# Down-projection weight sums: from VectorE through SBUF to copying and adding transfers within DRAM

## The chip, the cores and the metric

The kernel runs on one core of a Trainium2 chip. The metric is the device time of one execution in microseconds; the program uses only this core, so there is no slowest core to look for. Lower is better.

## The reference, cut to what matters

The program is a two-layer decoder trunk on a residual stream of 512 tokens by 1024 features in float32. Layer 0 has dilated windowed attention (12 heads in three groups, with rotary embedding), layer 1 has forgetting attention (16 heads, with keys and values computed once between the layers). Each is followed by a gated feed-forward block, and the change touches the last product of that block, the down-projection:

```python
def conv_ffn(xn, w_up, cw, cb, w_down):
    a = xn @ w_up
    T = a.shape[1]
    ap = jnp.pad(a, ((0, 0), (CONV_W - 1, 0), (0, 0)))
    a = sum(ap[:, j:j + T] * cw[j] for j in range(CONV_W)) + cb
    gate, val = jnp.split(a, 2, axis=-1)
    return (jax.nn.gelu(gate, approximate=True) * val) @ w_down     # (512, 2816) @ (2816, 1024)
```

## The kernel before

Every product is done in three float32r matmuls (high by high, high by low, low by high), so each weight piece of 128 x 1024 is loaded from DRAM by SyncE (`Weights.load`, L50), split into a high part on ScalarE and a low part on VectorE, and then used by TensorE. The emission order of the code is the order on each engine; nothing is rescheduled. A wait therefore holds up everything that stands behind it on the same engine's queue.

The down-projection works on eleven pairs `j` of 128-row chunks of `w_down[l]`, by a seven-product scheme (Strassen's, in Winograd's form): the 2 x 2 blocks of a pair (rows in two chunks of 128, columns in two halves of 512) are combined into four sums, the activations into matching sums (`pair_sums`, `pair_two`), and `combine_one` puts the products together. The weight sums don't depend on the data, so they are made long before they are used, and kept in a DRAM tensor `dT[l]` of 11 x 128 x 2048 floats. `down_sums` is a generator: each `next` emits one step of it.

* Before, one pair costs three loads into two SBUF tiles `dsums` (L615 to L617, SyncE), four subtractions of 128 x 512 on VectorE (L625) and two stores of 128 x 1024 to `dT` (L607, from SyncE or GpSimd).
* The steps stand between other work: the eleven pairs of layer 0 and pairs 6, 7 and 8 of layer 1 in the QKV stage of layer 0; pairs 0 to 5 of layer 1 in the stage that computes the shared keys and values; pairs 9 and 10 at the end of the forgetting attention.

Two places outside `down_sums` matter for the prediction:

* In the QKV stage, `wide_proj` makes one column group in four steps of weight pieces. After the last one `qk_post` scales the result on ScalarE and applies the rotary embedding on GpSimd, four instructions for each of four token blocks (L1139 to L1142). TensorE then transposes these blocks (`qk_transpose`, L1148).
* In the forgetting attention, `f_mask` (L1701) applies the causal mask to a bias tile on GpSimd; `f_exp` on VectorE (L1727) reads it, and `f_transpose` on TensorE (L1751) reads what comes out two units later. The first mask stands directly behind the last step of `down_sums` of the key and value stage on GpSimd's queue.

DMAs issued by SyncE (queue q1) and by GpSimd (queue q0) are carried by the same 16 DMA engines. GpSimd already issues adding transfers in the feed-forward blocks (`accum_op=ALU.add`, from one SBUF tile into another, L98 and L715), and the plain stores of `hD` (L671).

Of the kernel before, what the change touches and what calls it, by code (L numbers as in the profile page):

```python
# [13 lines left out]
ALU = mybir.AluOpType  # L14
# [16 lines left out]
ND = NF // 2  # L31
# [86 lines left out]
def trunk_kernel(ctx, tc, x, norm_gains, w_qkv_a, w_o_a, w_q_b, w_o_b, kv_norm, w_kvf, b_f,  # L118
# [11 lines left out]
    def t8(shape, dt=F32, name="t8"):  # L130
        return p8.tile(shape, dt, tag="t8", name=name)
# [22 lines left out]
    def add(f):  # L154
        pieces.append(f)
# [25 lines left out]
    def add_ffn(l):  # L181
        for c in range(NF):
            add_cols(w_up[l], c * 128)
            add_cols(w_up[l], DFF + c * 128)

        for j in range(ND):
            add(lambda raw, j=j: [(raw[:, 0:512], w_down[l][j * 256:j * 256 + 128, 0:512]),
                                  (raw[:, 512:1024], dT[l][j, :, 0:512])])
            add(lambda raw, j=j: [(raw, dT[l][j, :, 512:1536])])
        add_rows(w_down[l], range(1, NF, 2))  # L190

    add_rows(w_o_a[0], range(6))
# [403 lines left out]
        dve.tensor_copy(cp, pc)  # L596
        return cp

    def down_sums(pairs, place, queue, lag, behind, steps=False):


        live, n = [], len(pairs)

        def store(i):
            l, j = pairs[i]
            for q, t in enumerate(live[i]):
                queue.dma_start(dT[l][j, :, q * 1024:q * 1024 + 1024], t)  # L607

        for i in range(n + lag + behind):
            if i < n:  # L610
                l, j = pairs[i]
                a, b = place()
                live.append((a, b))
                r = w_down[l][j * 256:j * 256 + 256, :].rearrange("(c p) d -> c p d", p=128)
                sp.dma_start(a, r[0])  # L615
                sp.dma_start(b[:, 0:512], r[1, :, 512:1024])
                sp.dma_start(b[:, 512:1024], r[1, :, 0:512])  # L617
            single = steps and i - lag == n - 1
            if single:
                store(i - lag - behind)  # L620
            if 0 <= i - lag < n:
                a, b = live[i - lag]
                a0, a1, b0, b1 = a[:, 0:512], a[:, 512:1024], b[:, 0:512], b[:, 512:1024]
                for o, p, m in ((a0, a1, a0), (a1, b0, a1), (b0, b0, a0), (b1, b1, b0)):
                    dve.tensor_tensor(o, p, m, ALU.subtract)  # L625
                    if single and o is not b1:
                        yield
            if i >= lag + behind and not single:
                store(i - lag - behind)
            yield  # L630

    def in_one():
        t = t8([128, 2, 1024], name="dsums")
        return t[:, 0], t[:, 1]

    def in_two():
        return [t4([128, 1024], name="dsums") for _ in range(2)]

    def ffn(l, bd, cp, nxt, ahead):
        hD = tc.dram_tile([NF, 128, T], F32, name="hD")
# [144 lines left out]
        def pair_sums(j):  # L792

            pair_load(j + 1)
            k = acts[j]
            dve.tensor_tensor(k[:, s3_], k[:, a11], k[:, s1_], ALU.subtract)
            dve.tensor_tensor(k[:, s1_], k[:, s1_], k[:, s2_], ALU.add)
            dve.tensor_tensor(k[:, s2_], k[:, s1_], k[:, a11], ALU.subtract)
            pool.dma_start(sD[j], k[:, s2_])

# [11 lines left out]
        def load_two(j):  # L812

            if j < ND:
                later2[j] = k, r4 = t4([128, 768], name="dact2"), t2([128, 512], name="dt4")
                sp.dma_start(k[:, 0:256], sD[j])
                sp.dma_start(k[:, 256:768], hD[2 * j + 1])
                sp.dma_start(r4, dT[l][j, :, 1536:2048])
# [26 lines left out]
        def mul_one(j, bp):  # L845
            wa, wb, ac = [(t[:, 0], t[:, 1]) for t in one[j]]

            for key, q, w, c in (((bp, 0), 0, wa, H[0]), ((bp, 1), 3, wb, H[1]),
                                 ((bp + 2, 0), 2, wb, H[0]), ((bp + 2, 1), 1, wa, H[1])):
                if j == 0:  # L850
                    db[key] = bank([128, 512], name="acc")
                product_of(db[key], ac, q, w, c, bp, j == 0)

        def combine_one(bp):
            a, b, c, d = db[bp, 0], db[bp, 1], db[bp + 2, 0], db[bp + 2, 1]
            p1, u, u3 = (t2([128, 512], name="dsum") for _ in range(3))
            act.copy(p1, a)
            dve.tensor_tensor(u, b, p1, ALU.add)
            dve.tensor_tensor(c, c, u, ALU.add)
            act.copy(u3, c)  # L860
            dve.tensor_tensor(b, d, u, ALU.add)
            dve.tensor_tensor(d, d, u3, ALU.add)


        def p_11(j, bp, part=slice(0, 512)):
# [361 lines left out]
    def factors():  # L1227
# [9 lines left out]
        for _ in range(2):  # L1237
            next(down0)
# [193 lines left out]
    next(sums)  # L1432
# [18 lines left out]
    def v_post(g, b, o):  # L1451
        if b == 0:
            for i in (1, 2):
# [5 lines left out]
    v_proj0([[L(qk_transpose, 0, 0), L(qk_transpose, 0, 1), L(next, down0)],  # L1459
             [L(qk_transpose, 0, 2), L(qk_transpose, 0, 3), L(scores, 0, 0, 1), L(next, sums), L(next, down0)]])  # L1460
    wide_proj(1, "qk_ps", qk_post, [
        [],
        [L(scores, 0, 2, 3), L(next, sums)],
        [L(next, sums)],
        [stat_out, L(next, sums)]])
    wide_proj(2, "qk_ps", qk_post, [
        [L(next, sums)],
        [L(f, g, b) for f, g in ((p_transpose, 0), (qk_transpose, 1)) for b in range(4)],
        [L(scores, 1, 0, 1, 2, 3)],
        [exps, stat_in]])  # L1470
# [1 line left out]
    wide_proj(1, "v_ps", v_post, [  # L1472
        [L(qk_transpose, 2, 0), L(qk_transpose, 2, 1)],
        [L(qk_transpose, 2, 2), L(qk_transpose, 2, 3), L(scores, 2, 0, 1)],
        [L(next, down0), L(next, down0), L(scores, 2, 2, 3), factors],
        []], (0, 1, 3))
    pv(0, 0)
    for b in range(4):
        p_transpose(1, b)
# [120 lines left out]
    for sp_, b in [(sp_, b) for b in bd2.order for sp_ in (0, 2)]:  # L1600
# [14 lines left out]
    del wv  # L1615
    next(down1)

    bia = {}
# [39 lines left out]
    for c in range(8):  # L1658
        keys(c)
        for kc in range(2 * c, min(2 * c + 2, KD)):  # L1660
            if kc % 4 == 0:
                for part, name in zip(xTq, ("xqh", "xql")):
                    part.append(t8([128, 4, T], F32R, name=f"{name}{kc // 4}"))
            bd2.second(xTq, kc)
        if 1 <= c <= 5:
            next(gate)
        if c in (0, 1):
            next(down1)
# [139 lines left out]
    for n in range(N + 3):  # L1808
# [14 lines left out]
        if live:  # L1823
            if n + 1 < N:
                f_mask(*units[n + 1])
            if i == 1:
                q_low(j + 1)
            if i == 2 and j < 2 or (j, i) in ((6, 2), (7, 1)):
                W.low()
            if i == 3 and j:  # L1830
                f_out_low(j - 1)
            if i != 2:
                q_part(j + 1 + (i > 0), (i + 3) % 4)
            if (j, i) in ((7, 1), (7, 2)):
                next(down1)
        if 2 <= n < N + 2:
            f_transpose(*units[n - 2])
        if live and i == 1 and 2 <= j < 6:
# [19 lines left out]
    for _ in range(2):  # L1858
        next(down1)
    f_out_low(7)  # L1860
    W.ahead, W.ahead_dma = 4, 2
    cp = conv_columns(load_conv(1))
# [47 lines left out]
```

## Time and profile before

| | |
|---|---|
| time, median of 3 runs | 1097.54 us (1097.53 to 1097.63) |
| profiled execution: span | 1095.3 us |
| TensorE busy | 1088.0 us, 99% |
| TensorE weight loads busy | 946.4 us, 86% |
| VectorE busy | 882.3 us, 81% |
| ScalarE busy | 667.5 us, 61% |
| GpSimd busy | 154.4 us, 14% |
| DMA, of 16 engines' span | q1 (SyncE) 53.6%, q0 (GpSimd) 20.3% |

The profiled execution has no time of its own besides its span of 1095.3 us; the median of the runs stands 2.2 us above it, for what lies ahead of the first and behind the last instruction. The granted TensorE clock is 0.998 of full speed. GpSimd's DMA-issuing instructions are counted as its busy time; SyncE's are not.

### The profile page before, as it was taken

How to read it: one execution, taken by the hardware profiler on the slowest of the kernel's cores; microseconds unless marked ns; L12 is line 12 of the kernel's file. 1: busy time of each engine (PE TensorE's matmuls, PEld its weight loads, DVE VectorE, ACT ScalarE, POOL GpSimd, SP SyncE). 2: the span in 40 equal slices, each digit the busy share in tenths (PEclk: the TensorE clock that was granted, in tenths of full speed). 3: DMA queues.
4: the chain of work that ended last, by engine and by line, in shares of the span. 5: the costliest groups of instructions: out<-in, count | busy, mean ns of one | idle time of the engine just before them, and what ended most of it. 6: DMA issues, size and time to landing. Idle time of an engine off the chain costs nothing.

```text
span 1095.3 us, 17965 instructions
## 1 busy us (share of the span) xinstructions
PE 1088.0 (99%) x6537; PEld 946.4 (86%) x6537; DVE 882.3 (81%) x1510; ACT 667.5 (61%) x1117; POOL 154.4 (14%) x240
## 2 busy tenths in 40 slices
PE   9999999999999999999999999999999999999997
PEld 7888889899999988888878888889899999988886
DVE  5898979877878789897686667858878788779895
ACT  6745665656666656576451587755755656647473
POOL 2643000111111111000001212100111111211000
PEclk9999999999999999999999999999999999999999
DMA  9899944668898979793447867784568978979872
GB/s 292 241 366 405 351 125 135 135 164 198 190 210 190 226 266 325 268 341 99 146 143 240 274 174 207 243 238 136 105 174 190 213 184 184 245 244 318 313 250 77
DMA packets 191984, 241.60 MB, mean 221 GB/s; under 512 B 12832, under 2 KB 139160, under 8 KB 191896
## 3 DMA queue, kind: packets, MB, share of 16 engines
q1 hardware_dynamic: 176552, 189.33, 53.6%
q0 software_dynamic: 14656, 51.13, 20.3%
q8 instruction: 51, 0.84, 0.3%
q14 instruction: 37, 0.30, 0.1%
q10 hardware_dynamic: 688, 0.01, 0.1%
HBM read 172.37 MB, written 39.73 MB: 194 GB/s over the span
## 4 chain that ended last, share of the span: by engine, by line
PE 95%; DMA 2%; issue 1%; DVE 1%; ACT 0%; SPq 0%; DVEq 0%; ACTq 0%; POOL 0%; POOLq 0%
PE up L294 12%; PE up L292 12%; PE up L293 12%; PE acc L292 9%; PE acc L294 9%; PE acc L293 9%; PE v_ps L293 2%; PE v_ps L292 2%; PE v_ps L294 2%; PE pT_ps L1751 2%; PE o_ps L1766 2%; PE s_ps L1717 2%; PE qk_ps L292 1%; PE first L292 1%; PE first L293 1%; PE first L294 1%
## 5 line engine op out<-in xcount | busy, mean ns | idle before, releaser
L292 PE MATMUL acc<-w 128*128 128x512 f32 (+1 forms) x311 | 120.5, 388 | 0.0
L294 PE MATMUL acc<-w 128*128 128x512 f32 (+1 forms) x311 | 120.4, 387 | 0.0
L293 PE MATMUL acc<-w 128*128 128x512 f32 (+1 forms) x267 | 103.2, 387 | 0.0
L292 PE MATMUL up<-xsh,w 128*128 128x256 f32 x352 | 99.6, 283 | 0.0
L293 PE MATMUL up<-xsl,w 128*128 128x256 f32 x352 | 99.6, 283 | 0.0
L294 PE MATMUL up<-xsh,w 128*128 128x256 f32 x352 | 99.6, 283 | 0.0
L655 ACT ACTIVATE bb<-up,conv 128x512 f32<-128x512 f32 x80 | 59.7, 776 | 59.2 <-DVE up L1046 48.4
L60 ACT CAST w<-wraw 128x1024 fp32r<-128x1024 f32 x81 | 83.2, 1051 | 18.6 <-DMA wraw<-in_w_up_dram 7.8
L294 PE MATMUL up<-xch,w 128*128 128x512 f32 (+1 forms) x276 | 93.5, 339 | 0.1
L292 PE MATMUL up<-xbh,w 128*128 128x512 f32 (+1 forms) x276 | 93.6, 339 | 0.0
L293 PE MATMUL up<-xcl,w 128*128 128x512 f32 (+1 forms) x276 | 93.5, 339 | 0.0
L293 PE MATMUL up<-xbl,w 128*128 128x512 f32 (+1 forms) x276 | 93.5, 339 | 0.0
L292 PE MATMUL up<-xch,w 128*128 128x512 f32 (+1 forms) x276 | 93.5, 339 | 0.0
L294 PE MATMUL up<-xbh,w 128*128 128x512 f32 (+1 forms) x276 | 93.4, 338 | 0.0
L78 DVE TENSOR_TENSOR w<-wraw,w 128x1024 fp32r<-128x1024 f32 x62 | 74.6, 1223 | 16.6 <-ACT w L60 16.2
L292 PEld LDWEIGHTS acc<-w 128*128 128x128 f32 x311 | 58.4, 188 | 11.9
L294 PEld LDWEIGHTS acc<-w 128*128 128x128 f32 x311 | 58.4, 188 | 11.8
L292 PEld LDWEIGHTS up<-xsh,w 128*128 128x128 f32 x352 | 67.6, 192 | 0.0
L293 PEld LDWEIGHTS up<-xsl,w 128*128 128x128 f32 x352 | 67.6, 192 | 0.0
L294 PEld LDWEIGHTS up<-xsh,w 128*128 128x128 f32 x352 | 67.6, 192 | 0.0
L656 DVE SCALAR_TENSOR_TENSOR bb<-up,conv,bb 128x511 f32<-128x511 f32 x80 | 59.5, 744 | 7.9 <-ACT bb L655 7.8
L98 POOL DMA_DIRECT2D w<-wraw x20 | 17.5, 876 | 336.8 <-ACT w L71 307.3
(317 smaller groups left out, 3112.8 us busy)
## 6 DMA issues: line engine op xcount, KB each, us to landing
wraw<-in_w_up_dram SPq DMA_DIRECT2D x88, 512.0 KB
w<-wraw POOLq DMA_DIRECT2D x32, 512.0 KB, 6.2
dT<-dsums SPq DMA_DIRECT2D x28, 512.0 KB
dsums<-in_w_down_dram SPq DMA_DIRECT2D x22, 512.0 KB
dsums<-in_w_down_dram SPq DMA_DIRECT2D x44, 256.0 KB
w<-wsum POOLq DMA_DIRECT2D x22, 512.0 KB, 5.6
hD<-hc POOLq DMA_DIRECT2D x44, 256.0 KB, 7.2
dact<-hD SPq DMA_DIRECT2D x44, 256.0 KB
```

The source lines that it names most:

```text
L60: (copy or self.nc.scalar.copy)(pair[:, 0], raw)
L78: self.nc.vector.tensor_tensor(pair[:, 1], raw, pair[:, 0].bitcast(F32), ALU.subtract)
L98: self.nc.gpsimd.dma_start(pair[:, 1], raw, accum_op=ALU.add)
L292: pe.matmul(o, ah, bh, start=first, stop=False, skip_group_check=shared)
L293: pe.matmul(o, ah, bl, start=False, stop=False, skip_group_check=shared)
L294: pe.matmul(o, al, bh, start=False, stop=last, skip_group_check=shared)
L655: act.activation(bb[:, s, :], ps, AF.Identity, bias=cp[:, 3, ch:ch + 1], scale=cp[:, 2, ch:ch + 1])
L656: dve.scalar_tensor_tensor(bb[:, s, 1:], ps[:, :T - 1], cp[:, 1, ch:ch + 1], bb[:, s, 1:], ALU.mult, ALU.add)
L1717: pe.matmul(sc[j, i][hh][:, :nn], qT[j][own, qp, i * 128:(i + 1) * 128], k[own, kp, :nn], start=qp + kp == 0, stop=qp == 1)
L1751: pe.transpose(o[:, k0 + k, :], p[:, hh, k * 128:(k + 1) * 128], ident)
L1766: pe.matmul(o[64 * hh:64 * hh + 64, i * 128:(i + 1) * 128], Vt[hd // 8][:, k, (hd % 8) * 64:(hd % 8) * 64 + 64], pT[j, i, hh][:, k, :], st ...
```

## The change

The sums are no longer made on VectorE. For each pair, two transfers of SyncE copy the four blocks from `w_down` straight into the four sections of `dT`, one of the blocks twice (`twice` reads it with a step of zero). Three adding transfers of GpSimd then finish the sums within DRAM: the second block of the first chunk is added into sections 0 and 3, section 3 into section 2, and section 2 into section 1. Each is one step of the generator later than the one that it depends on, so pair `i` takes steps `i` to `i + 3`, and eleven pairs take 14 steps. The transfers add where VectorE subtracted, so two of the sums have the opposite sign, and the activations' sums and `combine_one` are changed to match. The sections of `dT` change places accordingly. All pairs of layer 0 are now made in the QKV stage (14 steps), all of layer 1 in the key and value stage (14 steps), and the steps at other places are gone.

```diff
-    def down_sums(pairs, place, queue, lag, behind, steps=False):
+    def twice(a):
+        return bass.AP(tensor=a.tensor, offset=a.offset, ap=[a.ap[0], [0, 2], a.ap[1]])
+
+    def down_sums(pairs):
+        n = len(pairs)
+        sums = [dT[l][j].rearrange("p (s c) -> p s c", c=512) for l, j in pairs]
+
+        def rows(i, c):
             l, j = pairs[i]
...
-                a, b = place()
-                live.append((a, b))
-                r = w_down[l][j * 256:j * 256 + 256, :].rearrange("(c p) d -> c p d", p=128)
-                sp.dma_start(a, r[0])
-                sp.dma_start(b[:, 0:512], r[1, :, 512:1024])
-                sp.dma_start(b[:, 512:1024], r[1, :, 0:512])
...
-                for o, p, m in ((a0, a1, a0), (a1, b0, a1), (b0, b0, a0), (b1, b1, b0)):
-                    dve.tensor_tensor(o, p, m, ALU.subtract)
...
+            return w_down[l][j * 256 + c * 128:j * 256 + c * 128 + 128, :]
+
+        for i in range(n + 3):
             if i < n:
+                sp.dma_start(sums[i][:, 0::2], twice(rows(i, 0)[:, 0:512]))
+                sp.dma_start(sums[i][:, 1::2], rows(i, 1).rearrange("p (s c) -> p s c", c=512))
+            if 0 <= i - 1 < n:
+                pool.dma_start(sums[i - 1][:, 0::3], twice(rows(i - 1, 0)[:, 512:1024]), accum_op=ALU.add)
+            if 0 <= i - 2 < n:
+                pool.dma_start(sums[i - 2][:, 2], sums[i - 2][:, 3], accum_op=ALU.add)
+            if i - 3 >= 0:
+                pool.dma_start(sums[i - 3][:, 1], sums[i - 3][:, 2], accum_op=ALU.add)
             yield
...
-            dve.tensor_tensor(k[:, s1_], k[:, s1_], k[:, s2_], ALU.add)
+            dve.tensor_tensor(k[:, s1_], k[:, s1_], k[:, s2_], ALU.subtract)
...
-            dve.tensor_tensor(k[:, 0:256], k[:, 256:512], k[:, 0:256], ALU.subtract)
+            dve.tensor_tensor(k[:, 0:256], k[:, 256:512], k[:, 0:256], ALU.add)
...
-    sums = down_sums([(1, 6), (1, 7)], in_two, sp, 1, 3)
...
-    down0 = down_sums([*[(0, j) for j in range(ND)], (1, 8)], in_one, sp, 1, 1, True)
+    down0 = down_sums([(0, j) for j in range(ND)])
...
-    down1 = down_sums([(1, j) for j in range(6)], in_two, pool, 1, 0)
+    down1 = down_sums([(1, j) for j in range(ND)])
...
-    down1 = down_sums([(1, 9), (1, 10)], in_one, pool, 2, 0)
```

The number of matmuls and their order on TensorE are the same. What moves is on GpSimd, SyncE and VectorE. On GpSimd in the QKV stage, before, the rotary embedding of column group 1 (`qk_811`) follows directly on the casts of the stage's beginning, and that of group 2 (`qk_1126`) directly on that:

```order
L1122 CAST xph_142<-xah_138 128x16x32
L1122 CAST xpl_144<-xal_140 128x16x32
L1139 TENSOR_TENSOR rope<-qk_811,rope 128x128
L1140 TENSOR_TENSOR rope<-qk_811,rope 128x8x8
L1141 TENSOR_TENSOR rope<-qk_811,rope 128x8x8
L1142 TENSOR_TENSOR qk_811<-rope 128x8x16
```

Now (the same instructions have the lines L1101 and L1118 to L1121, the groups the names `qk_770` and `qk_1061`, and `dT_75` is `dT` of layer 0) nine adding transfers stand ahead of group 1, and twelve more between group 1 and group 2, of which these are the last six:

```order
L618 DMA dT_75<-in_w_down_dram 128x2x512
L620 DMA dT_75<-dT_75 128x512
L622 DMA dT_75<-dT_75 128x512
L618 DMA dT_75<-in_w_down_dram 128x2x512
L620 DMA dT_75<-dT_75 128x512
L622 DMA dT_75<-dT_75 128x512
L1118 TENSOR_TENSOR rope<-qk_1061,rope 128x128
```

So group 2's rotary embedding now stands behind transfers that each wait for an earlier one.

At the other place, between the feed-forward block of layer 0 and the first mask of the forgetting attention, GpSimd before issues twelve stores of finished sums, behind the feed-forward block's stores of `hD` and `sD` (`dT_76` is `dT` of layer 1; a count at the end of a row stands for equal rows in succession):

```order
L799 DMA sD<-dact 128x256
L671 DMA hD<-hc 128x512
L1080 DMA hD<-hc 128x512
L799 DMA sD<-dact 128x256 x7
L607 DMA dT_76<-dsums 128x1024 x12
L1701 AFFINE_SELECT bias<-bias 128x2x128 x11
```

Now it issues 33 adding transfers there, and the masks (now L1676) follow them; these are the last rows:

```order
L618 DMA dT_76<-in_w_down_dram 128x2x512
L620 DMA dT_76<-dT_76 128x512
L622 DMA dT_76<-dT_76 128x512
L620 DMA dT_76<-dT_76 128x512
L622 DMA dT_76<-dT_76 128x512 x2
L1676 AFFINE_SELECT bias<-bias 128x2x128 x11
```

The first mask now stands behind the last of 33 adding transfers, where it stood behind a store. On SyncE, the 22 copies of this stage stand between the loads of the key and value weights, the last two pairs of them behind the four stores `cd<-rel`, which wait for VectorE.

More of the change, by code (lines that the diff above doesn't have):

```diff
@@ L188, in add_ffn @@
                                   (raw[:, 512:1024], dT[l][j, :, 0:512])])
-            add(lambda raw, j=j: [(raw, dT[l][j, :, 512:1536])])
+            add(lambda raw, j=j: [(raw, dT[l][j, :, 1024:2048])])
         add_rows(w_down[l], range(1, NF, 2))
@@ L597, in conv_columns @@
         return cp
-    def down_sums(pairs, place, queue, lag, behind, steps=False):
-        live, n = [], len(pairs)
-        def store(i):
+    def twice(a):
[4 more added lines that the diff above has]
+        def rows(i, c):
             l, j = pairs[i]
-            for q, t in enumerate(live[i]):
-                queue.dma_start(dT[l][j, :, q * 1024:q * 1024 + 1024], t)
-        for i in range(n + lag + behind):
+            return w_down[l][j * 256 + c * 128:j * 256 + c * 128 + 128, :]
+        for i in range(n + 3):
@@ L610, in down_sums @@
             if i < n:
-                l, j = pairs[i]
-                a, b = place()
-                live.append((a, b))
-                r = w_down[l][j * 256:j * 256 + 256, :].rearrange("(c p) d -> c p d", p=128)
-                sp.dma_start(a, r[0])
-                sp.dma_start(b[:, 0:512], r[1, :, 512:1024])
-                sp.dma_start(b[:, 512:1024], r[1, :, 0:512])
[L618 to L623, printed above, removed]
-                for o, p, m in ((a0, a1, a0), (a1, b0, a1), (b0, b0, a0), (b1, b1, b0)):
-                    dve.tensor_tensor(o, p, m, ALU.subtract)
-                    if single and o is not b1:
-                        yield
@@ L628, in down_sums @@
-            if i >= lag + behind and not single:
-                store(i - lag - behind)
-            yield
[L632 to L637, printed above, removed]
+                sp.dma_start(sums[i][:, 0::2], twice(rows(i, 0)[:, 0:512]))
+                sp.dma_start(sums[i][:, 1::2], rows(i, 1).rearrange("p (s c) -> p s c", c=512))
+            if 0 <= i - 1 < n:
+                pool.dma_start(sums[i - 1][:, 0::3], twice(rows(i - 1, 0)[:, 512:1024]), accum_op=ALU.add)
@@ L817, in load_two @@
                 sp.dma_start(k[:, 256:768], hD[2 * j + 1])
-                sp.dma_start(r4, dT[l][j, :, 1536:2048])
+                sp.dma_start(r4, dT[l][j, :, 512:1024])
         def pair_two(j):
@@ L846, in mul_one @@
             wa, wb, ac = [(t[:, 0], t[:, 1]) for t in one[j]]
-            for key, q, w, c in (((bp, 0), 0, wa, H[0]), ((bp, 1), 3, wb, H[1]),
-                                 ((bp + 2, 0), 2, wb, H[0]), ((bp + 2, 1), 1, wa, H[1])):
+            for key, q, w, c in (((bp, 0), 0, wa, H[0]), ((bp, 1), 3, wb, H[0]),
+                                 ((bp + 2, 0), 2, wb, H[1]), ((bp + 2, 1), 1, wa, H[1])):
                 if j == 0:
@@ L860, in combine_one @@
             act.copy(u3, c)
-            dve.tensor_tensor(b, d, u, ALU.add)
-            dve.tensor_tensor(d, d, u3, ALU.add)
+            dve.tensor_tensor(b, d, u, ALU.subtract)
+            dve.tensor_tensor(d, d, u3, ALU.subtract)
         def p_11(j, bp, part=slice(0, 512)):
@@ L1236, in factors @@
         act.activation(f, f, AF.Exp)
-        for _ in range(2):
-            next(down0)
         dve.tensor_tensor(w, l, f, ALU.mult)
@@ L1430, in trunk_kernel @@
     reorder(act.copy, 2, 3, parts=(0,))
-    sums = down_sums([(1, 6), (1, 7)], in_two, sp, 1, 3)
-    next(sums)
     def wide_proj(g, name, post, between, sums=range(4)):
@@ L1456, in v_post @@
         act.activation(V[2][:, b, :], o[:, 256:512], AF.Identity, scale=factor(2, b))
-    down0 = down_sums([*[(0, j) for j in range(ND)], (1, 8)], in_one, sp, 1, 1, True)
+    down0 = down_sums([(0, j) for j in range(ND)])
     v_proj0([[L(qk_transpose, 0, 0), L(qk_transpose, 0, 1), L(next, down0)],
-             [L(qk_transpose, 0, 2), L(qk_transpose, 0, 3), L(scores, 0, 0, 1), L(next, sums), L(next, down0)]])
+             [L(qk_transpose, 0, 2), L(qk_transpose, 0, 3), L(scores, 0, 0, 1), L(next, down0)]])
     wide_proj(1, "qk_ps", qk_post, [
         [],
-        [L(scores, 0, 2, 3), L(next, sums)],
-        [L(next, sums)],
-        [stat_out, L(next, sums)]])
+        [L(scores, 0, 2, 3)],
+        [],
+        [stat_out]])
     wide_proj(2, "qk_ps", qk_post, [
-        [L(next, sums)],
+        [],
         [L(f, g, b) for f, g in ((p_transpose, 0), (qk_transpose, 1)) for b in range(4)],
@@ L1474, in trunk_kernel @@
         [L(qk_transpose, 2, 2), L(qk_transpose, 2, 3), L(scores, 2, 0, 1)],
-        [L(next, down0), L(next, down0), L(scores, 2, 2, 3), factors],
-        []], (0, 1, 3))
+        [L(scores, 2, 2, 3), factors],
+        []])
     pv(0, 0)
@@ L1615, in trunk_kernel @@
     del wv
+    next(down1)
     next(down1)
@@ L1666, in trunk_kernel @@
             next(gate)
-        if c in (0, 1):
-            next(down1)
+        next(down1)
         if c == 6:
@@ L1833, in trunk_kernel @@
                 q_part(j + 1 + (i > 0), (i + 3) % 4)
-            if (j, i) in ((7, 1), (7, 2)):
-                next(down1)
         if 2 <= n < N + 2:
@@ L1856, in trunk_kernel @@
             W.load(W.n_dma + 1)
-    for _ in range(2):
-        next(down1)
     f_out_low(7)
```

## Prediction

> **What bounds the kernel now.** First the page, for the engines over the whole span.
>
> ```profile
> PE 1088.0 (99%) x6537; PEld 946.4 (86%) x6537; DVE 882.3 (81%) x1510; ACT 667.5 (61%) x1117; POOL 154.4 (14%) x240
> DMA  9899944668898979793447867784568978979872
> ```
>
> TensorE (PE) is busy for 1088.0 of 1095.3 us. The second row is the busy share of the 16 DMA engines in 40 slices of 27.4 us: 8 or 9 tenths in the first five slices (the QKV stage), 3 to 4 tenths in slices 18 to 20 and 7 to 8 in 21 and 22 (the key and value stage). Next the waits of TensorE, to see whether anything off it costs time now.
>
> ```profile
> PE warm L246 <- DVE zero L241: 1.2, 1, 1.2
> PE v_ps L293 <- DVE w L82: 0.2, 1, 0.2
> ```
>
> Behind the start, TensorE waited 0.2 us for VectorE in the whole run. So VectorE's 81% is hidden, and freeing it can give back next to nothing. The question is whether the new transfers stay hidden. For that I read where GpSimd's and the DMA engines' work meets TensorE: the chain of waits at the two places where TensorE takes what GpSimd made, the timelines of GpSimd and VectorE there, and the DMA queues in those stretches.
>
> ```profile
> 104.59 0.87 PE qkT_ps L1148 x8
> 621.97 0.37 PE pT_ps L1751 x2
> ```
>
> At 104.59 TensorE transposes the first two blocks of column group 2; at 621.97 the first probabilities of the forgetting attention. Neither waits now.
>
> **What is removed.** Per pair four subtractions; their group is this row (least, median and longest ns).
>
> ```profile
> L625 DVE TENSOR_TENSOR dsums<-dsums x88: 669/692/948, 47.6 to 712.6; 128x512 f32<-128x512 f32 x88
> ```
>
> 88 x 0.69 = 61 us leave VectorE, worth at most the 0.2 us that TensorE waited for it. The turned signs (`pair_sums`, `pair_two`, `combine_one`, the columns in `mul_one`) keep count and shape of every instruction: nothing. The loads and stores of `dsums` go too; they are credited below, stage by stage.
>
> **What a transfer costs.** I count in units of 512 KB (0.524 MB) and in time of all 16 DMA engines. Before, a pair was two units of load and two of store. Now it is two units of copy within DRAM (price c each) and two of adding within DRAM: one whole, two halves (price a each). The trace has neither, so each gets bounds. Plain transfers first: in 63 to 101 us only loads and stores ran, queue q1 alone; in 510 to 618 us q0 carried twelve stores alone.
>
> ```profile
> q1 hardware_dynamic: 6286, 15.05, 103.1%
> ...
> q1 hardware_dynamic: 15348, 15.16, 46.2%
> q0 software_dynamic: 1728, 6.29, 15.1%
> ```
>
> 15.05 MB in 1.031 x 38 = 39.2 us is 1.36 us a unit; the stores took 0.151 x 108 = 16.3 us for 12 units, 1.36 us again. For the adding, 300 to 320 us holds three transfers that add from SBUF into SBUF and two half-unit stores:
>
> ```profile
> q0 software_dynamic: 592, 2.10, 55.9%
> ...
> w<-wsum POOLq DMA_DIRECT2D x2, 512.0 KB, 5.6
> w<-wraw POOLq DMA_DIRECT2D x1, 512.0 KB, 6.2
> hD<-hc POOLq DMA_DIRECT2D x2, 256.0 KB, 7.7
> ```
>
> 0.559 x 20 = 11.2 us, less 1.36 for the stores, is 3.3 us a unit: 2.4 times a plain one. So c is at least 1.36 us, if reading and writing DRAM overlap as a load's two sides do, and at most 2.7, if a load's time and a store's follow each other; neither row is nearer, so I take the middle, 2.0. And a is at least 3.3, if DRAM serves as well as SBUF, and at most 3.3 + 1.36 = 4.7, if DRAM adds a plain unit's time; the row is itself an adding transfer, so I stay near it: 3.5. A gain is excluded, since the same bytes are read and written whatever the place.
>
> That GpSimd issues the adding doesn't bring it engines of its own: the 103.1% above is all 16 engines, taken by SyncE's queue alone. The Trainium skill, DMA: Bandwidth & Descriptors, section Issuing engines are not separate DMA queues, says the same of transfers issued from several engines; by that rule, a stage that was full of plain transfers has no place for adding ones from another queue. The same page, section Latency and other measured facts, gives 207 to 214 GB/s for copies between HBM tensors; an estimate from it is c = 2.5 us, with which the sum below would be 65 us instead of 50. No row of this trace shows such a copy.
>
> **The key and value stage.** Here GpSimd has 33 adding transfers in front of the first mask, and its queue is in order.
>
> ```profile
> 611.19 0.53 POOL L607 DMA_DIRECT2D dT<-dsums  x1 [1.09 <-DVE dsums L625]
> 611.72 2.20 POOL L1701 TENSOR_SCALAR_AFFINE_SELECT bias<-bias 128x256 f32<-128x256 f32 x3
> ...
> 615.65 0.29 DVE L1727 CUSTOM_DVE_ANT_0 prob<-s_ps,bias 128x128 f32<-128x128 f32 x1 [2.00 <-PE s_ps L1717]
> ...
> 617.11 0.48 DVE L1739 TENSOR_SCALAR prob<-prob,rl 128x128 f32<-128x128 f32 x2
> ```
>
> The mask of 611.72 is read at 615.65, normalized by 617.6, and TensorE wants it at 621.97. So the mask can come about 6 us later, at 617.7, for nothing. SyncE reaches the first copies no earlier than 510, behind five loads that wait for their buffers:
>
> ```profile
> 489.88 20.60 SPq L50 DMA_DIRECT2D wraw<-in_w_kvf_dram  x5
> 510.57 0.53 SPq L615 DMA_DIRECT2D dsums<-in_w_down_dram  x1
> ```
>
> What the DMA engines do between 510 and 618 us: 46.2% + 15.1% of 108 us, 66.2 us. Of it leave the twelve stores (16.3 us) and the loads of six pairs, 12 units (16.3 us); 33.6 us of weights and biases stay. About 8 us of those (an estimate: half of the five query weights and the larger biases) stand behind the last copies and needn't be over, so 26 us are in front. To them come 22c + 22a:
> - 2.0 and 3.5: 26 + 121 = 147 us, end at 657, 39 us past 617.7;
> - 1.36 and 3.3: 26 + 102.5 = 128.5 us, end at 638.5, 21 us past;
> - 2.7 and 4.7: 26 + 163 = 189 us, end at 699, 81 us past.
>
> Weights behind the copies on SyncE's queue come late too, but that is the same engines' time and isn't added again. What is late next, should the mask be on time, are the bias loads, which stand behind all copies.
>
> **The QKV stage.** The rotary embedding of groups 1 and 2 now stands behind 9 and 12 adding transfers.
>
> ```profile
> 43.47 1.14 POOL L1122 CAST xpl<-xal 128x512 fp32r<-128x512 f32 x1
> 67.10 0.92 POOL L1139 TENSOR_TENSOR rope<-qk,rope 128x128 f32<-128x128 f32 x1 [22.49 <-ACT qk L1133]
> ...
> 98.09 0.46 POOL L1139 TENSOR_TENSOR rope<-qk,rope 128x128 f32<-128x128 f32 x1 [18.14 <-ACT qk L1133]
> ...
> 100.83 0.91 POOL L1139 TENSOR_TENSOR rope<-qk,rope 128x128 f32<-128x128 f32 x1
> ...
> 104.04 0.46 POOL L1139 TENSOR_TENSOR rope<-qk,rope 128x128 f32<-128x128 f32 x1
> ...
> 105.55 0.47 POOL L1139 TENSOR_TENSOR rope<-qk,rope 128x128 f32<-128x128 f32 x1
> ...
> 200.47 1.05 POOL L98 DMA_DIRECT2D w<-wraw  x1 [92.98 <-ACT w L71]
> ```
>
> The first nine (6.5 units) can begin at 44.6, behind the last cast, and have until 67.1: 6.5 x 3.5 = 22.8 us, which fits. Group 2 is the tight one. Its first two blocks, from 98.09, were done 0.5 us before TensorE took them at 104.59. The third block took 1.5 us (104.04 to 105.55) where the first took 2.7 (98.09 to 100.83); with the subtractions gone I count 1.6 for each, so the start may slip to 101.4. Between the end of group 1, about 74, and that, twelve transfers (8 units) stand on GpSimd, each waiting for one of the step before. The last 1.5 units need only be issued, so 6.5a must pass, and up to 8c of copies for the next pairs share the engines:
> - 74 + 6.5 x 3.5 + 8 x 2.0 = 113, 11 us past 101.4;
> - least, with the copies gone ahead: 74 + 21.5 = 95.5, nothing;
> - most: 74 + 30.6 + 21.6 = 126, 25 us past.
>
> Behind group 2, twelve more wait for nobody: GpSimd's next work in the feed-forward block begins at 200.47, after 93 us of idling.
>
> **The sum.** 39 + 11 = 50 us, between 21 and 106. The profiled execution goes from 1095.3 to 1145 us, and the median of the runs, 2.2 us above it, from 1097.5 to 1148 us.
>
> **The rivals.**
> - Hidden, so not slower. If an engine reads for an adding transfer while it writes for a copy, the two queues' times don't add up. The stage of 108 us holds everything from c + a = (108 - 26) / 22 = 3.7 us on downward, where a and c one after the other are 4.7 at least. For it: TensorE waits nowhere now, and the weights have several steps of lead. Against it: the 103.1% with which full stretches stop. Time: 1097.5. Chance 0.08, with 0.01 of it for a gain.
> - Faster by VectorE's relief alone. TensorE's idle behind its start is under 1 us, so 1097.0 at best; over 0.2% (2.2 us) would need waits that the profile doesn't have. Chance 0.02.
> - The adding is held up by DRAM, row by row, instead of by bytes: a at twice the SBUF row, 6.6 us. Then 26 + 22 x 8.6 = 215 us in the key stage (107 us past), and 74 + 43 + 16 = 133 (32 past) in the QKV stage: 1237 us. For it: a unit that adds already costs 2.4 plain ones. Against it: that an addition reads both its operands explains 2 of the 2.4. Chance 0.14.
> - The change doesn't do what it says, if the copies with the step of zero fell into many short pieces. The rows stay 2 KB, and the 6286 packets of 15.05 MB above are of that size; I give it no chance of its own.
>
> **How the numbers follow.** The forecast, a wait at one or both places of 21 to 106 us, has 0.76: 1118 to 1204. To hold 8 in 10 the range reaches down toward the hidden case: 1106 to 1204. What a measurement can tell from no change is 0.2%, 2.2 us. Faster: 0.03 (0.01 + 0.02). Within 0.2%: 0.07 (the rest of the hidden case). Slower: 0.90.
>
> **What would show it.** In the profile after: TensorE's waits name GpSimd or its rotary embedding and mask, some 10 us near 105 and 40 us near 620; VectorE is down by 61 us; GpSimd's waits are for DMAs, on the lines of the adding transfers; the DMA row is at 9 in slices 19 to 22; q0's share rises from 20.3% by (44 x 3.5 - 16 x 1.36) / 1095, about 12 points. I am wrong if TensorE stays at 99%, if a unit that adds takes under 2 us, or if the waits are at another place, such as the weights.

## The result and the profile after

The changed kernel takes 1169.45 us (median of 4 runs, 1160.73 to 1172.21) where the kernel before, measured beside it, takes 1097.53 (1097.25 to 1097.63): a ratio of 1.0642, with a 95% interval of 1.0602 to 1.0681. It is slower by 72 us. Its four runs spread over 11.5 us, so a difference of a few us from it says little. The profiled execution has a span of 1170.4 us, 75.1 us more than before.

The page of the changed kernel, engines, slices and the queue that carries the additions:

```profile
PE 1107.2 (95%) x6537; PEld 955.8 (82%) x6537; DVE 821.6 (70%) x1422; ACT 667.6 (57%) x1117; POOL 199.4 (17%) x290
...
PEclk9998899999999999999997779999999999999999
DMA  9999994478888979778999986754467888988961
...
q0 software_dynamic: 24672, 65.81, 30.9%
```

VectorE lost 882.3 - 821.6 = 60.7 us of work, and nothing came of it. TensorE's busy time rose by 1107.2 - 1088.0 = 19.2 us with the same 6537 instructions, and its idle time from 7.3 to 63.2 us, by 55.9. 19.2 + 55.9 = 75.1, the whole difference, as busy and idle time must. So TensorE waits, and it works slower for a while after it has waited; what the second part adds to the loss is taken up below. What it waited for:

```profile
PE qkT_ps L1127 <- POOL qk L1121: 18.8, 2, 18.4
PE q_ps L292 <- ACT w L60: 14.2, 2, 9.9
PE v_ps L292 <- ACT w L60: 13.0, 3, 7.4
PE s_ps L1692 <- ACT qst L1622: 5.5, 1, 5.5
```

The first row is the rotary embedding of group 2 (the QKV stage). The next two are weights of the key and value stage that came late (ScalarE copies them as soon as they land). Only the last, 5.5 us, stands behind the mask: ScalarE's copy of the query (`qst`) stands behind exponentials that need it. The places, from the table of stretches (engine columns as in the prediction, then TensorE's granted clock, the DMA engines' share and GB/s):

```profile
101.00:150.00 49.00, 30.16 (x192) 24.41 (x192) 16.66 (x58) 19.15 (x67) 18.17 (x28) 0.83 1.09 207
150.00:200.00 50.00, 47.31 (x289) 38.68 (x285) 35.60 (x51) 31.97 (x59) 4.09 (x5) 0.97 0.72 173
...
560.00:618.00 58.00, 54.63 (x241) 43.79 (x239) 30.69 (x41) 19.97 (x28) 15.17 (x16) 1.00 1.05 197
618.00:660.00 42.00, 26.31 (x77) 18.67 (x78) 6.11 (x6) 4.97 (x6) 8.61 (x9) 0.72 1.05 192
660.00:700.00 40.00, 24.39 (x106) 18.27 (x105) 11.82 (x37) 10.86 (x25) 8.11 (x13) 0.79 0.90 182
```

TensorE's gaps in the five rows are 18.8, 2.7, 3.4, 15.7 and 15.6 us: 21.5 in the QKV stage, 34.7 in the key and value stage. In 101 to 150 and from 560 to 700 the DMA engines are full or nearly so (1.09, then 1.05, 1.05, 0.90). The timeline at the two places:

```profile
44.41 2.45 POOL L618 DMA_DIRECT2D dT<-in_w_down_dram  x2
...
74.24 0.87 POOL L1118 TENSOR_TENSOR rope<-qk,rope 128x128 f32<-128x128 f32 x1
...
121.00 0.74 POOL L1118 TENSOR_TENSOR rope<-qk,rope 128x128 f32<-128x128 f32 x1
...
122.86 1.11 PE L1127 MATMUL qkT_ps<-ident,qk 128*128 128x128 f32 x4 [18.45 <-POOL qk L1121]
...
536.37 0.58 SPq L615 DMA_DIRECT2D dT<-in_w_down_dram  x1
...
589.86 19.18 SPq L615 DMA_DIRECT2D dT<-in_w_down_dram  x1
...
618.92 0.80 PE L292 MATMUL q_ps<-xqh,w 128*128 128x512 f32 x1 [4.29 <-ACT w L60]
...
690.90 1.41 POOL L1676 TENSOR_SCALAR_AFFINE_SELECT bias<-bias 128x256 f32<-128x256 f32 x3
...
691.64 0.29 DVE L1702 CUSTOM_DVE_ANT_0 prob<-s_ps,bias 128x128 f32<-128x128 f32 x1 [13.30 <-POOL bias L1676]
...
695.60 0.69 PE L1726 MATMUL pT_ps<-ident,prob 128*128 128x128 f32 x2
```

Group 2's rotary embedding starts at 121.0 instead of 98.1; the first probabilities are transposed at 695.6 instead of 622.0. VectorE waited 13.3 us for the first mask, up to 691.6, and TensorE's 5.5 us fall into that time. SyncE reached the first copy of layer 1 at 536.4, where before it reached the first load for the sums of this stage at 510.6: the QKV stage had already cost 26 us by then. Later one copy kept SyncE's queue for 19.2 us (the row of 589.86); theory B below starts from that.

### The profile page after: what moved, and what is told of

Read it like the earlier page. It is cut to its first block, busy times and chain, and to the rows that moved or that the text cites. A ratio compares the mean times of both kernels' runs of the same rounds, so it can differ in the third digit from the quotient of the medians.

```text
span 1170.4 us, 17769 instructions
## 1 busy us (share of the span) xinstructions
PE 1107.2 (95%) x6537; PEld 955.8 (82%) x6537; DVE 821.6 (70%) x1422; ACT 667.6 (57%) x1117; POOL 199.4 (17%) x290
## 4 chain that ended last, share of the span: by engine, by line
PE 76%; DMA 13%; SPq 7%; ACT 2%; issue 1%; DVE 1%; POOL 0%; DVEq 0%; POOLq 0%; ACTq 0%
PE up L293 12%; PE up L292 12%; PE up L294 12%; PE acc L292 7%; PE acc L294 7%; PE acc L293 7%; DMA dT<-in_w_down_dram 6%; SPq L615 3%; DMA wraw<-in_w_qkv_a_dram 3%; SPq L616 2%; DMA wraw<-in_w_o_a_dram 2%; PE qk_ps L1338 2%; PE pT_ps L1726 2%; PE o_ps L1741 2%; PE s_ps L1692 1%; PE first L292 1%
## 6 DMA issues: line engine op xcount, KB each, us to landing
dT<-in_w_down_dram POOLq DMA_DIRECT2D x22, 512.0 KB, 14.7
```

## The experiments

Theory A is that of the prediction: the 16 DMA engines are one shared resource, an addition takes 2 to 3 times a plain transfer's time on them, and all that needs them at those places comes late, weights as well as what stands behind the additions on GpSimd. Theory B blames SyncE's queue, where weights stand behind copies; theory C GpSimd's queue, where each addition waits for the landing of an earlier one and the rotary embedding and the mask stand behind. Theory D is that an addition mostly waits, so that other transfers fit beside it.

**Without the additions** (`adds_out`):

```
-            if 0 <= i - 1 < n:
-                pool.dma_start(sums[i - 1][:, 0::3], ..., accum_op=ALU.add)
-            ...
```

> The changed kernel without its 66 adding transfers (the weight sums stay unfinished); the 44 copies and everything behind them stay. Theory A (the time of the 16 DMA engines is the cause, a copy costs about 2.0 us a unit and an addition 3.5 to 3.8): the key and value stage holds 26 + 22 x 2.0 = 70 us in 108, the QKV stage has no adding in front of the rotary embedding; TensorE waits for nothing and the time is 1097.5 to 1100 us. Theory B (the copies hold SyncE's queue, so that weights behind them are issued late, whatever the adding does; issues of copies took up to 19 us each in the changed kernel's trace): weights stay late by 20 us or more, 1118 us or more. Theory C (the GpSimd's queue alone, each adding transfer waiting for the landing of the one before): 1097.5 us as in A.

Measured: 1097.5 us, ratio 1.0003 (0.9993 to 1.0012). The 44 units of copies and the freed VectorE together change nothing. Its DMA queue between 510 and 618 us:

```profile
q1 hardware_dynamic: 18685, 20.66, 60.2%
```

All 22 units of copies are in this row, with the weights, and it is 60%. So the copies alone leave room, and theory B falls as an explanation of its own: the same copies on the same queue delay nobody when the additions are missing. That SyncE's queue stands still behind them beside the additions is one of the ways in which the lack of the engines' time reaches the weights.

**The additions made plain** (`adds_plain`):

```
-                pool.dma_start(sums[i - 1][:, 0::3], twice(...), accum_op=ALU.add)
+                pool.dma_start(sums[i - 1][:, 0::3], twice(...))
 (and the same for the two half-unit ones)
```

> The changed kernel with its 66 adding transfers turned into plain ones of the same shapes, on the same queue of GpSimd, in the same order, with the same waits and the same bytes written; only the addition is left out (so the sums are not sums). Theory A (time of the DMA engines, of which the addition takes 3.3 to 3.8 us a unit and a copy 1.4 to 1.6, as the run without additions showed): the key and value stage holds 26 + 22 x (1.5 + 1.5) = 92 us in 108, the QKV stage is at 74 + 6.5 x 1.5 + 8 x 1.5 = 96 us where 101 is wanted: 1097 to 1101 us. Theory C (the chain of waits and landings on GpSimd's queue, whatever the transfers do): 1130 us or more.

Measured: 1106.3 us, ratio 1.0071 (1.0054 to 1.0088). Of the 72 us 63 go when the same 66 transfers no longer add. Their queue between 510 and 620 us:

```profile
q0 software_dynamic: 3069, 10.66, 38.3%
```

0.383 x 110 = 42.1 us for 10.66 / 0.524 = 20.3 units is 2.07 us a unit. The same transfers adding, in the changed kernel between 536 and 691 us:

```profile
q0 software_dynamic: 5994, 11.25, 53.2%
q1 hardware_dynamic: 17660, 19.86, 50.2%
```

0.532 x 155 = 82.5 us for 21.5 units, 3.84 us a unit. The order, the waits and the bytes written were the same, so theory C in its pure form, the chain whatever the transfers do, falls. An addition also lands later than its plain twin (medians of 15.1 and 13.5 us against 10.0 and 9.5), which makes the same chain longer; this run doesn't separate that from the engines' time. The weights that came late stand behind no addition on GpSimd's queue, and `dve_posts` below takes the chain out of TensorE's way. The run was 5 us slower than A's upper figure: a plain unit costs 2.07 in this company, not the 1.5 I had put in.

**The prices alone** (`probe`): the kernel before, with transfers of the same shapes behind its last store.

```
+    for j in range(8):
+        copy(1, j)            # as L615 and L616
+    for j in range(7, -1, -1):
+        whole(1, j)           # as L618
+    for j in range(8):
+        pool.dma_start(part(1, j)[:, 2], part(1, j)[:, 3], accum_op=ALU.add)
+    ...                       # then 8 whole(1, j) beside 4 copy(0, j)
```

> The kernel before, with transfers added behind its last store, where the DMA engines are idle: 8 pairs of copies (16 units) alone; then 8 adding transfers of a whole unit and 8 of half a unit alone; then 8 whole adding transfers on GpSimd's queue while SyncE copies 4 pairs (8 units). Theory A: copies 1.36 to 1.6 us a unit, 22 to 26 us; additions 3.3 to 3.8, 26 to 30 us and 13 to 15; together the sum, 8 x (3.3 to 3.8) + 8 x (1.36 to 1.6) = 37 to 43 us. Theory D (an adding transfer waits more than it uses, so that copies go in its gaps): together no longer than the additions alone, 26 to 30 us.

Measured: 1225.7 us (one run); the prices are in its trace, behind the end of the kernel before. Its DMA queues in four stretches: copies alone (1100 to 1118 us), whole additions alone (1130 to 1150), halves alone (1156 to 1168), copies and additions at once (1186 to 1210):

```profile
q1 hardware_dynamic: 3036, 5.85, 106.1%
...
q0 software_dynamic: 1806, 3.48, 105.2%
...
q0 software_dynamic: 1053, 1.90, 97.8%
...
q0 software_dynamic: 1133, 2.17, 57.5%
q1 hardware_dynamic: 1692, 3.25, 46.4%
```

Share times length over units: a copy takes 1.061 x 18 / 11.2 = 1.71 us a unit, a whole addition 1.052 x 20 / 6.64 = 3.17, the halves 0.978 x 12 / 3.63 = 3.24. At once they take 3.33 (addition) and 1.79 (copy), and the two shares sum to 104%. Each costs within 5% of what it costs alone and they share the engines' time, so theory D falls and the prices add up: 8 x 3.33 + 8 x 1.79 = 41 us for the last set, inside theory A's 37 to 43. (The 16 units of copies alone come to 27 us, just above its 22 to 26, and the eight whole additions to 25, just under its 26 to 30.) The Trainium skill, DMA: Bandwidth & Descriptors, section Issuing engines are not separate DMA queues, says that transfers issued from several engines run on the same 16 DMA engines and interleave there; the 57.5% and 46.4% agree.

**One layer at a time** (`layer0_only`): layer 1 takes layer 0's sums and makes none.

```
-    dT = [tc.dram_tile([ND, 128, 2048], F32, name=f"dT{l}") for l in range(2)]
+    dT = [tc.dram_tile([ND, 128, 2048], F32, name="dT")] * 2
...
-    down1 = down_sums([(1, j) for j in range(ND)])
+    down1 = down_sums([])
...
```

> The changed kernel with the weight sums of layer 1 left out altogether (its down-projection takes those of layer 0); layer 0 as changed. It splits the 72 us. In the changed kernel's trace SyncE reached the first copy of layer 1 at 536.4 us where before it was there at 510.6, so the QKV stage should account for 26 us: 1121 to 1126 us, and the key and value stage for the other 46 to 49. If the stages lean on each other (a backlog of the first that the second pays for), it is under 1115.

Measured: 1122.4 us, ratio 1.0233 (1.0217 to 1.0248). The QKV stage costs 1122.4 - 1097.2 = 25 us, the key and value stage, by subtraction, the other 47. The waits of TensorE in this run, and the engines on its page:

```profile
PE qkT_ps L1127 <- POOL qk L1121: 19.9, 2, 19.5
```

```profile
PE 1092.5 (97%) x6537; PEld 949.1 (85%) x6537; DVE 821.6 (73%) x1422; ACT 667.9 (60%) x1117; POOL 168.8 (15%) x257
```

TensorE idles 1121.3 - 1092.5 = 28.8 us, 21.5 more than before, and its work takes 4.5 us longer. The gaps in its QKV stage are thus the same 21.5 us as in the changed kernel. For the key and value stage that leaves 55.9 - 21.5 = 34.4 us of waits and 19.2 - 4.5 = 14.7 us of slower work.

**GpSimd's queue out of the way** (`dve_posts`): the rotary embedding of groups 1 and 2 and the masks on VectorE.

```
-        pool.tensor_tensor(tu[:, 0], qk[:, :, 0:16], c2, ALU.mult)
+        eng = dve if g else pool
+        eng.tensor_tensor(tu[:, 0], qk[:, :, 0:16], c2, ALU.mult)
 ...
-        pool.affine_select(d, d, ...)
+        dve.tensor_tensor(d, d, mask0[:, None, 128:256].to_broadcast([128, 2, 128]), ALU.add)
```

> The changed kernel with the rotary embedding of groups 1 and 2 and the causal masks of the forgetting attention done by VectorE, so that no work for TensorE stands behind adding transfers on GpSimd; transfers as changed. Theory A (time of the DMA engines): the weights behind the same transfers are late anyway. The last weights of the QKV stage landed at 119.2 us, so TensorE, that waited until 122.9 for the rotary embedding, waits for weights instead and gains 4 to 14 us; in the key and value stage the query projection ended at 681 and the first probabilities could follow at 686 instead of 695.6, a gain of some 10: 1145 to 1156 us. Theory C (the order on GpSimd's queue is the cause): nearly all of the loss is gone, 1098 to 1115 us.

Measured: 1163.1 us, ratio 1.0594 (1.0561 to 1.0627): 6 us less, where A expected 14 to 24 and C 54 to 71. The runs of the two kernels overlap (1159.5 to 1166.6 against 1160.7 to 1172.2), so even the 6 us aren't clear of their spread. What TensorE waited for:

```profile
PE pT_ps L1189 <- ACT V L1432: 14.6, 1, 14.6
PE q_ps L292 <- ACT w L60: 13.5, 2, 11.3
PE v_ps L292 <- ACT w L60: 12.5, 3, 7.9
PE qkT_ps L1128 <- ACT qk L1112: 5.7, 1, 5.7
```

Where it had waited 18.8 us for the rotary embedding it now waits 5.7 + 14.6 us for ScalarE: the copies of the results (`qk`, `V`) stand there behind the splitting of weights, and ScalarE waited 14.0 us for weights of this stage and 17.1 us for one of the next. The wait for GpSimd covered another one of nearly the same length. In the key and value stage the first probabilities came at 689.6 instead of 695.6. So theory C falls as the cause; what A expected to gain was too hopeful, and a gain is not shown.

**Without the copies of layer 1** (`copies1_out`):

```
-    dT = [tc.dram_tile([ND, 128, 2048], F32, name=f"dT{l}") for l in range(2)]
+    dT = [tc.dram_tile([ND, 128, 2048], F32, name="dT")] * 2
...
-            if i < n:
+            if i < n and pairs[i][0] == 0:
                 sp.dma_start(sums[i][:, 0::2], ...)
...
```

> The changed kernel without the copies of layer 1 (its 22 units; both layers share one set of sums, so that layer 1 adds onto those of layer 0); all adding transfers stay. Theory A (time of the DMA engines): the QKV stage stays late by about 26 us; the key and value stage holds 26 + 22 x 3.8 = 110 us in 108, the mask is late by 0 to 5 us: 1123 to 1129 us. Theory C (the chain on GpSimd: 13 steps, each waiting for a landing of 13 to 16 us, as the changed kernel's trace shows under load): 13 x 13 = 169 us from the first addition, 30 to 60 us past the mask's time whether copies run or not: 1150 to 1185 us. Theory B (SyncE's queue held by copies): no copies hold it here, 1123 us.

Measured: 1178.5 us, ratio 1.0744 (1.0728 to 1.0761). A's number missed it. It lies in C's range of 1150 to 1185, but by luck, not for C's reason, because the edit did more than I had thought: the copies were also what the additions waited for, and without them GpSimd began the additions at 471.4 instead of 547.2, among the loads of layer 0's down-projection. From its waits and its timeline:

```profile
PE acc L292 <- ACT w L811: 40.3, 7, 10.9
```

```profile
ACT w L810 <- DMA dt<-dT: 67.4, 16, 10.8
```

```profile
590.77 0.81 POOL L622 DMA_DIRECT2D dT<-dT  x1 [4.55 <-DMA dT<-dT]
670.99 0.41 POOL L1676 TENSOR_SCALAR_AFFINE_SELECT bias<-bias 128x256 f32<-128x256 f32 x1 [79.41 <-DMA bias<-cd]
```

The last addition is out at 590.8; the mask comes 79 us later and waits for its bias. So GpSimd's chain held up no mask here. TensorE instead waited 40.3 us for operands of the product that the additions ran beside: ScalarE splits them right behind the weight sums (`dt`), for whose loads it waited 67.4 us. That speaks for A, though the run doesn't separate the copies' share as it was meant to.

**The additions where there is room** (`adds_spread`, `adds_spread2`): copies as changed, the same 66 additions issued later.

```
+    for _ in adds_of(0): pass                            # behind group 2's rotary embedding
...
+        if c >= 2: next(adds1)                           # key loop: six whole ones
...
+            if i == 3 or j > 4 and i == 1: next(adds1)   # between heads: eleven
...
+                if l == 1: next(adds1, None)             # up-projection: sixteen
```

> The changed kernel with the same copies at the same places and the same 66 adding transfers, but these issued where the DMA engines have room: all of layer 0 behind the last rotary embedding of the QKV stage, those of layer 1 six in the key and value stage, eleven between the heads of the attention and sixteen in the up-projection of layer 1. Theory A: 22 units x 3.3 to 3.8 are 73 to 84 us a layer, and the run without additions left the DMA engines idle for 29 us in 101 to 150, 36 us in 150 to 200 and some 20 of every 100 us after: 1097 to 1104 us. If an adding transfer holds up others wherever it runs (weights and biases late by some us at each), 1115 us or more.

Measured: 1132.8 us, ratio 1.0317 (1.0295 to 1.0339); a miss by some 30 us. The largest waits:

```profile
PE xt_ps L376 <- DVE xn L326: 24.7, 1, 24.7
PE pT_ps L1747 <- ACT prob L1725: 3.1, 1, 3.1
```

What ScalarE waited for, and the stretch, with the columns of the table above:

```profile
ACT w L60 <- DMA wraw<-in_w_up_dram: 26.8, 5, 11.0
```

```profile
150.00:200.00 50.00, 24.90 (x105) 20.15 (x104) 20.20 (x32) 16.98 (x35) 14.53 (x18) 0.73 0.85 170
```

Layer 1's loss is nearly gone (3.1 us are left of it), layer 0's has moved: 22 units in one stretch behind the rotary embedding kept the DMA engines at 0.97 from 101 to 150 and at 0.85 from there to 200, ScalarE waited 26.8 us for the first weights of the up-projection, and as its queue is in order, the next norm, which stands behind their splitting, came 25 us late. I had counted the idle time of the DMA engines as if nothing else wanted it in the same moment. The second version thins out layer 0:

```
+    for _ in range(ND): next(adds[0])                    # only the eleven whole ones
...
+                for _ in range(1 + (c % 3 == 0)): next(adds[l], None)   # 22 halves in each up-projection
```

> As the spread version, but thinner: of layer 0 only the eleven whole additions stand behind the last rotary embedding, and the 22 halves follow in the up-projection of layer 0, one or two behind each column block; of layer 1 six whole ones in the key and value stage, five between the heads, and the 22 halves in the up-projection of layer 1. Theory A: eleven units at 3.2 us (the probe's price) are 35 us, where the run without additions left 65 us of the DMA engines' time idle between 101 and 200, so the 24.7 us that TensorE waited behind the o-projection go, and each half costs 1.6 us in stretches with 15 to 35% idle: 1097 to 1104 us. Rival: an addition anywhere holds up what runs beside it, and the loss only moves into the up-projections: 1115 us or more. Faster than before by over 2 us is not expected of any, since TensorE waits for nothing there.

Measured: 1104.9 us, ratio 1.0070 (1.0057 to 1.0082). Its page, and what TensorE waited for:

```profile
PE 1091.3 (99%) x6537; PEld 947.3 (86%) x6537; DVE 821.5 (74%) x1422; ACT 667.4 (60%) x1117; POOL 199.7 (18%) x290
...
q0 software_dynamic: 24672, 65.81, 30.5%
```

```profile
PE xt_ps L376 <- DVE xn L326: 2.1, 1, 2.1
PE pT_ps L1747 <- ACT prob L1725: 1.9, 1, 1.9
```

The same 66 additions, and GpSimd's queue still takes 0.305 x 1103.7 = 337 us of the engines' time, against 0.309 x 1170.4 = 362 in the changed kernel; yet 65 of the 72 us are gone. What the additions cost is thus mostly a matter of place. No version beat the kernel before, and none here could by much: TensorE is at 99% in it too, and freeing VectorE gave nothing.

## Why the prediction was right, and where it was not

The forecast was 1148 us, within 1106 to 1204; measured were 1169. The mechanism was the one forecast, additions that take the DMA engines' time in the two stages, and both stages came out longer than their sums, so no error hid another.

- **VectorE's relief is worth at most 0.2 us.** Right: 60.7 us went, and with the additions out the time is 1.0003 of before.
- **The prices.** I took c = 2.0 within 1.36 to 2.7; alone it is 1.71. I took a = 3.5 within 3.3 to 4.7; alone it is 3.17 to 3.24, just under the SBUF row, so DRAM adds as fast as SBUF, and 3.84 in the key and value stage. The Trainium skill's figure for copies (DMA: Bandwidth & Descriptors, Latency and other measured facts), from which I estimated 2.5, is given there for rows of 16 KiB at pitches of 512 KiB and more, which the prediction left out. It doesn't fit the rows of 2 KB here: the probe moved 5.85 MB in 18 us, 325 GB/s.
- **The rival "hidden"** needed c + a of 3.7 or less; it is 4.9 at least, and the probe's shares add up. **The rival "row by row"** needed 6.6 for an addition; it is at most half of that alone.
- **The QKV stage: 11 us predicted, 25 measured.** The step that failed is the sum for the first nine, "6.5 x 3.5 = 22.8 us, which fits". (It didn't quite fit by its own figures either: from 44.6 to 67.1 are 22.5 us.) They took from 44.4 to 74.2, 29.8 us, because the copies and weights of the same stretch share the engines: from 40 to 75 us queue q1 took 56.0% of them and the additions 48.1%. I had charged the copies only in front of group 2. From there the sum held: 38.75 us predicted between the groups, 81.3 to 121.0, 39.7, measured. So the start of group 2 slipped to 121 instead of 113; TensorE waited 21.5 us in the stage instead of 11, and its slower work behind the wait added 4.5.
- **The key and value stage: 39 us predicted, 47 measured.** The stage's 147 us became 690.9 - 536.4 = 154.5. The term that was too small is a: with 3.84 in place of 3.5 the sum 26 + 22 x (2.0 + a) gives the 154.5. (Copies and weights together cost 0.502 x 155 us for 37.9 units, 2.05 a unit, in that stage. That the 26 us held was not measured by itself.) The mask came at 690.9, 73.2 us past 617.7; less the 26 us of the QKV stage this is the 47.
- **What would show it.** I named the mask as what TensorE would wait for near 620, for 40 us. It was the weights, 27 us, and the mask 5.5; I had said myself that waits at the weights would make me wrong, so as a signature it was wrong. The path was right: the mask still came last (VectorE waited 13.3 us for it). And the text had the right sentence, that weights behind the copies are late by the same engines' time and not in addition; `dve_posts` bears it out, for taking the mask and the rotary embedding off GpSimd gave back some 6 us of 72, and these are not clear of the spread. The DMA row is at 9 in slices 19 to 22, counted from 0, as forecast. VectorE's 61 us were right (60.7), and q0 nearly so: 0.309 x 1170.4 - 0.203 x 1095.3 = 139 us more, where I had put 132.
- **A term that the sum didn't have** is TensorE's clock after a wait. The same matmul then takes longer for a while:

```profile
629.53 0.79 PE L292 MATMUL v_ps<-w,xkh 128*128 128x512 f32 x1 [4.75 <-ACT w L60]
...
633.95 0.63 PE L294 MATMUL v_ps<-w,xkl 128*128 128x512 f32 x1
...
635.06 0.39 PE L294 MATMUL v_ps<-w,xkl 128*128 128x512 f32 x1
```

```profile
629.50:634.80 5.30, 4.80 (x10) 3.43 (x11) 1.23 (x1) 0.00 (x0) 1.67 (x2) 0.50 1.03 170
634.80:639.50 4.70, 4.70 (x21) 3.60 (x19) 0.00 (x0) 0.00 (x0) 0.00 (x0) 0.99 1.00 194
```

The granted clock is 0.50 for 5.3 us and then 0.99: ten matmuls in the first row, 21 in the shorter second. The Trainium skill, TensorE: Matmul & The Clock Gate, Part 1: The HAM clock gate (the "warmup" mystery), gives half rate after an idle window and full rate again about 4 us into steady work. The trace agrees roughly: behind each of the six waits of over 4 us in the changed kernel TensorE works at 0.50 for 3.4 to 6.4 us. There is a seventh such stretch, of 3.4 us, behind three waits of only 0.7 us in succession (171 to 174 us). TensorE is busy for 32 us in the seven together; at half rate 16 of these are lost, most of the 19.2 us of slower work (an estimate from the granted clock of these stretches).

It would be wrong to add the 19.2 us to the loss as a second cause. In the key and value stage TensorE's slower work up to 686 us lies in front of the wait for the mask, and the mask's time comes from the DMA engines; with a faster TensorE that wait would have been longer by as much. This is argued from the trace; no run separates it. What isn't covered so is the 4.5 us in the QKV stage and some 3 us behind 693.4 (half of the 6.1 us for which TensorE is busy from 693.3 to 699.7 at 0.50). The page of before had no wait from which to read this, but a forecast of 50 us of waits in pieces should have had a small term for it.

What stays open: why an addition costs 3.84 us in the key and value stage and 3.2 alone, when in the probe a copy beside it raised it only to 3.33. A plain unit costs about a fifth more in that stage too (2.07 on GpSimd's queue, against 1.71 for a copy alone), so it may not be something of the additions only. The small packets of the bias loads in that stage are a candidate; no run separates them.

## What to carry to other kernels

Moving arithmetic from an idle-enough engine into adding transfers trades a hidden cost for DMA time: here, for each layer, 22 units went from 1.36 us (a load) to 1.71 (a copy) and 22 from 1.36 (a store) to 3.2 (an addition). So count the engine-time of the stretch before and after, and count everything that shares it from the first transfer on. Which wait the profile names then says little of the cause: with the DMA engines full, all that needed them here was late together, and freeing one queue uncovered the next wait. If such transfers must be issued, thin them out over stretches with room (65 of 72 us here), and charge a wait of TensorE of over 4 us with some 2.5 us more for the clock (half of about 5 us at 0.50), where no later wait swallows it.

## What the runs showed of the hardware that was not expected

- Adding within DRAM costs no more than adding within SBUF: 3.17 to 3.24 us per 512 KB against the 3.3 read from before. A copy within DRAM costs 1.71, a quarter more than a load.
- Copies and additions from two queues at once nearly keep their prices (1.79 and 3.33, alone 1.71 and 3.17) and split the engines' time, 46.4% and 57.5%.
- TensorE's granted clock was 0.50 for 3.4 to 6.4 us of work behind each of the six waits of over 4 us, and once for 3.4 us behind three waits of 0.7 us close together.
